# Two heads' scores on the two halves of the array's rows, one scan of 1280 columns per head, and W_in's chunks split 1024 columns at a time

## The chip, the core and the metric

The kernel runs on one core of one Trainium2 chip. The metric is the time of one execution on the device in microseconds (us); lower is better. Five engines work in parallel, each through its own list of instructions in order: PE (matmuls and transposes), ACT (activations and copies), DVE (elementwise arithmetic and scans), POOL (here masks and a few small things) and SP, which issues the DMAs. They wait for each other on semaphores only.

## What is computed

One layer of a decoder trunk with 512 tokens, width 1024, 8 heads of 64, in float32. Only the attention matters here. `q`, `k`, `v` are columns of `h @ w_in`, and each head weighs its values by stick breaking:

```python
z = einsum('bhqd,bhkd->bhqk', q, k) * 64 ** -0.5
causal = key_pos < q_pos                       # strictly
log_beta = log_sigmoid(z)
log_keep = where(causal, log_beta - z, 0.0)    # log(1 - beta)
between = cumsum(log_keep, reverse=True) - log_keep
w = where(causal, exp(log_beta + between), 0.0)
y = einsum('bhqk,bhkd->bhqd', w, v)
```

So a weight is its own `beta` times the product of all `keep = 1 - beta` that lie to its right in the same row, up to the diagonal.

## The kernel before

**Numbers in two parts.** PE reads a rounded float32 type. Every operand x of a matmul is therefore split (`split`, L63 to L66) into a high part, which ACT casts (line L64), and a low part, x minus the high one, which DVE subtracts (L65). A product is three matmuls (`mm3`, L89): high times high (L90), high times low (L91), low times high (L92).

**Weights.** W_in comes in chunks of 1024 rows by 128 columns (`wcols`). SP loads a chunk into one of 4 buffers `raw` (L71). `weights` then splits it in two halves, so ACT runs two casts `whi` of 128x512 and DVE two subtractions `wlo` of 128x512. The parts lie in a pool `wts` of 15 buffers; one that is taken again waits for whoever read or saved it last. A projection (`proj`) is 8 times 3 matmuls of 512 columns into one of the 8 PSUM banks.

**Order.** PE's and SP's lists are in the order in which the program is written (`manual_schedule`). ACT's, DVE's and POOL's lists are put in order by the framework's scheduler when the program is built.

**The attention.** The loop at L424 runs over j = 0 to 3, two heads each, which I call pair j, with heads a and b. In order, PE does: the scores of both heads, two projections for the convolution (`conv_u`, `conv_b`), the transposes of head a's weights (`wtrans`, L366), the next pair's q projection, the transposes of head b's weights, the next pair's k projection, the products with v (`av`, L380) and the next `conv_c` projection.

**Scores before** (`scores`, called once per head). `proj_q` and `proj_k` leave, for each head, a tile `st` whose 128 rows hold q's 64 high values above its 64 low values (swapped for head b), and k's high parts twice and k's low parts twice. One matmul over 128 rows thus gives two of the products, and two matmuls (L338, L339) give all four. The causal part of the scores is four blocks `BLK` of 512, 384, 128 and 256 columns, 1280 in all, in three PSUM banks. ACT takes `beta` (L341) and `keep` (L342) out of each bank. POOL sets the diagonal blocks (L347). Then, block by block, DVE forms the running product of `keep` from right to left (L350) and multiplies it into `beta` (L351), one column shifted. For each projection of k, ACT copies four pieces of 64x512 (L325) and DVE subtracts four (L326); for q two and two (L315 to L318).

**Other work in this stage.** `make_sums` loads pieces of another weight, DVE forms sums (L308), and SP saves them to DRAM (`wsum`, L291), in this stage between W_in's loads.

Of the kernel before, what the change touches and what calls it, by code (L numbers as in the profile page):

```python
# [16 lines left out]
P = 128  # L17
# [16 lines left out]
def hybrid_block(ctx, tc, x, p, g_pre_mix, w_in, b_gate, w_conv, w_attn_out, w_conv_out, w_o,  # L34
# [19 lines left out]
    def bigt(shape, dt=F32R, name="big"):  # L54
        return big.tile(shape, dt, tag="big", name=name)
# [12 lines left out]
    def weights(loads, shape):  # L68
        raw = raws.tile(shape, F32, tag="raw", name="raw")
        for sel, src in loads(raw):  # L70
            nc.sync.dma_start(sel, src)  # L71
        lo = wts.tile(shape, F32R, tag="w", name="wlo")
        hi = wts.tile(shape, F32R, tag="w", name="whi")
        half = shape[1] // 2
        for sl in (slice(0, half), slice(half, 2 * half)):
            split(hi[:, sl], lo[:, sl], raw[:, sl])
        return hi, lo
# [233 lines left out]

    def proj_q(j):
        a, b = st = [bigt([P, 3, S], name="st") for _ in range(2)]
        ps = proj(wcols(w_in, j * P), hx)
        nc.scalar.copy(a[0:64, 0], ps[0:64])  # L315
        nc.vector.tensor_tensor(a[64:128, 0], ps[0:64], a[0:64, 0].bitcast(F32), op=ALU.subtract)
        nc.scalar.copy(b[64:128, 0], ps[64:128])
        nc.vector.tensor_tensor(b[0:64, 0], ps[64:128], b[64:128, 0].bitcast(F32), op=ALU.subtract)  # L318
        return st

    def proj_k(j, st):
        ps = proj(wcols(w_in, 512 + j * P), hx)
        for s_, r, o in ((st[0], slice(0, 64), slice(64, 128)), (st[1], slice(64, 128), slice(0, 64))):
            for d in (r, o):
                nc.scalar.copy(s_[d, 1], ps[r])  # L325
                nc.vector.tensor_tensor(s_[d, 2], ps[r], s_[r, 1].bitcast(F32), op=ALU.subtract)  # L326

    def scores(st):
        beta = bigt([P, 1280], F32, "beta")
        keep = bigt([P, 1280], F32, "keep")  # L330
        for group in ((3,), (2, 0), (1,)):
            ps = bank()
            base = BLK[group[0]][0]
            for qb in group:
                c0, n = BLK[qb]
                c0 -= base
                lhs = st[:, 0, qb * P:(qb + 1) * P]
                nc.tensor.matmul(ps[:, c0:c0 + n], lhs, st[:, 1, 0:n], start=True, stop=False)  # L338
                nc.tensor.matmul(ps[:, c0:c0 + n], lhs, st[:, 2, 0:n], start=False, stop=True)  # L339
            n = sum(BLK[qb][1] for qb in group)  # L340
            nc.scalar.activation(beta[:, base:base + n], ps[:, 0:n], AF.Sigmoid, scale=0.125)  # L341
            nc.scalar.activation(keep[:, base:base + n], ps[:, 0:n], AF.Sigmoid, scale=-0.125)  # L342
        for qb in (3, 2, 0, 1):
            c0, n = BLK[qb]
            dg = slice(c0 + n - P, c0 + n)
            for t_, fill in ((beta, 0.0), (keep, 1.0)):
                nc.gpsimd.affine_select(t_[:, dg], t_[:, dg], pattern=[[-1, P]], compare_op=ALU.is_gt,  # L347
                                        fill=fill, base=0, channel_multiplier=1)
            kr = keep[:, c0:c0 + n][:, ::-1]
            nc.vector.tensor_tensor_scan(kr, kr, kr, 1.0, op0=ALU.mult, op1=ALU.bypass)  # L350
            nc.vector.tensor_tensor(beta[:, c0:c0 + n - 1], beta[:, c0:c0 + n - 1], keep[:, c0 + 1:c0 + n],  # L351
                                    op=ALU.mult)
# [71 lines left out]
    for j in range(4):  # L424
        wa = scores(st[0])
        wb = scores(st[1])
# [482 lines left out]
```

## Time and profile before

| what | value |
|---|---|
| time, median of 3 runs | 736.56 us (735.95 to 737.09) |
| time of the profiled execution | 737.48 us |
| its span, first to last instruction | 735.7 us |
| PE busy | 727.5 us, 99% of the span |
| DVE, ACT, POOL busy | 538.4, 392.4, 89.2 us |
| TensorE's granted clock | 1.000 |

How to read it: the profile is one execution. Its span is the time from the first to the last instruction; 1.8 us of the execution's own time lie around it. Start times are counted from the span's start. A row of the timeline holds start, length, engine, line, operation, out<-in by the program's names, and in brackets the idle time of the engine before it and who ended it. A matmul's length reaches until its result can be used; the next one starts earlier, so the distance of the starts is PE's pace.

### The profile page before, as it was taken

Reading aid. Unit: us, or ns where it says so; the run is one execution under the profiler, and the core shown is the slowest. Engines: PE = TensorE matmul, PEld = TensorE weight load, DVE = VectorE, ACT = ScalarE, POOL = GpSimd, SP = SyncE. Lnnn points to the kernel's source line nnn. Section 1 sums busy time; section 2 is a strip of 40 time slices with the busy share of each in tenths; the row PEclk is TensorE's granted clock in tenths of the full one; section 3 lists DMA queues with packets and bytes.
Section 4 is the critical chain, followed back from the end, with each engine's and each line's share of the span. In section 5 each row is a group of like instructions: output and inputs, shape, how many; then the busy total and the mean of one; then the engine's idle time right before and its main releaser. Section 6 shows DMA issues by size and latency. Waiting matters only on the chain.

```text
span 735.7 us, 10417 instructions
## 1 busy us (share of the span) xinstructions
PE 727.5 (99%) x3944; PEld 631.4 (86%) x3944; DVE 538.4 (73%) x740; ACT 392.4 (53%) x647; POOL 89.2 (12%) x119
## 2 busy tenths in 40 slices
PE   8999999999999999999999999999999999999997
PEld 7878888888888888888899999999988888888886
DVE  6779898989545533844789898976799878269762
ACT  6264746373434221443856696757767477256431
POOL 1005041323332222001100000000000000001100
PEclk9999999999999999999999999999999999999999
DMA  8591717174798967862325544523555767577311
GB/s 314 170 290 57 218 40 229 62 224 141 234 341 256 279 207 261 296 216 70 152 94 170 176 115 115 148 81 107 153 171 178 219 249 226 177 242 270 128 57 58
DMA packets 112106, 132.29 MB, mean 180 GB/s; under 512 B 4116, under 2 KB 82744, under 8 KB 111032
## 3 DMA queue, kind: packets, MB, share of 16 engines
q1 hardware_dynamic: 111464, 127.43, 54.8%
q10 hardware_dynamic: 592, 4.20, 1.4%
q8 instruction: 31, 0.51, 0.3%
q14 instruction: 19, 0.16, 0.1%
HBM read 108.55 MB, written 23.07 MB: 179 GB/s over the span
## 4 chain that ended last, share of the span: by engine, by line
PE 85%; DVE 6%; DMA 5%; issue 1%; ACT 1%; SPq 0%; POOL 0%; POOLq 0%; DVEq 0%; ACTq 0%
PE ps L90 27%; PE ps L92 27%; PE ps L91 26%; DMA raw<-in_w_up_dram 3%; DMA raw<-in_w_in_dram 2%; DVE us L65 2%; PE ps L380 1%; PE ps L366 1%; PE ps L339 1%; PE ps L181 1%; PE ps L338 1%; PE ps L565 1%; PE ps L140 0%; DVE s L660 0%; DVE wlo L65 0%
## 5 line engine op out<-in xcount | busy, mean ns | idle before, releaser
L65 DVE TENSOR_TENSOR wlo<-raw,whi 128x512 fp32r<-128x512 f32 x120 | 84.8, 737 | 42.7 <-ACT whi L64 20.9
L90 PE MATMUL ps<-h1h,whi 128*128 128x512 f32 x288 | 113.0, 392 | 0.0
L92 PE MATMUL ps<-h1h,wlo 128*128 128x512 f32 x288 | 112.3, 390 | 0.0
L91 PE MATMUL ps<-h1l,whi 128*128 128x512 f32 x288 | 112.2, 390 | 0.0
L64 ACT CAST whi<-raw 128x512 fp32r<-128x512 f32 x120 | 68.9, 630 | 48.5 <-DMA raw<-in_w_in_dram 15.8
L90 PE MATMUL ps<-w,sb 128*128 128x512 f32 x216 | 84.1, 389 | 0.0
L92 PE MATMUL ps<-w,sb 128*128 128x512 f32 x216 | 84.0, 389 | 0.0
L91 PE MATMUL ps<-w,sb 128*128 128x512 f32 x216 | 84.0, 389 | 0.0
L65 DVE TENSOR_TENSOR w<-raw,w 128x1024 fp32r<-128x1024 f32 x56 | 67.6, 1221 | 21.5 <-ACT w L64 10.4
L64 ACT CAST w<-raw 128x1024 fp32r<-128x1024 f32 x56 | 58.4, 1052 | 36.1 <-DMA raw<-wsum 14.4
L132 POOL TENSOR_TENSOR rs<-ms,mhalf 128x1 f32<-128x1 f32 x20 | 14.2, 712 | 419.6 <-DVE ms L128 365.7
L90 PE MATMUL ps<-h2h,us 128*128 128x256 f32 x224 | 63.5, 283 | 0.4 <-DVE tmp L692 0.4
L92 PEld LDWEIGHTS ps<-h1h,wlo 128*128 128x128 f32 x288 | 54.1, 188 | 11.3
L91 PEld LDWEIGHTS ps<-h1l,whi 128*128 128x128 f32 x288 | 54.1, 188 | 10.8
L91 PE MATMUL ps<-h2l,us 128*128 128x256 f32 x224 | 63.4, 283 | 0.0
L92 PE MATMUL ps<-h2h,us 128*128 128x256 f32 x224 | 63.4, 283 | 0.0
L90 PEld LDWEIGHTS ps<-h1h,whi 128*128 128x128 f32 x288 | 54.1, 188 | 10.8
L65 DVE TENSOR_TENSOR us<-raw,us 128x1024 fp32r<-128x1024 f32 x42 | 50.6, 1219 | 5.9 <-ACT us L64 5.8
L64 ACT CAST us<-raw 128x1024 fp32r<-128x1024 f32 x42 | 43.3, 1049 | 17.0 <-DVE raw L664 8.5
L91 PEld LDWEIGHTS ps<-w,sb 128*128 128x128 f32 x216 | 40.6, 188 | 8.4
L92 PEld LDWEIGHTS ps<-w,sb 128*128 128x128 f32 x216 | 40.6, 188 | 8.4
L90 PE MATMUL ps<-tb,us 128*128 128x256 f32 x168 | 47.7, 284 | 0.0
(210 smaller groups left out, 1693.1 us busy)
## 6 DMA issues: line engine op xcount, KB each, us to landing
raw<-in_w_in_dram SPq DMA_DIRECT2D x36, 512.0 KB, 6.5
w<-in_w_down_dram SPq DMA_DIRECT2D x32, 512.0 KB, 4.5
wsum<-w SPq DMA_DIRECT2D x32, 512.0 KB, 4.1
raw<-in_w_up_dram SPq DMA_DIRECT2D x32, 512.0 KB, 4.6
raw<-wsum SPq DMA_DIRECT2D x32, 512.0 KB, 5.0
raw<-in_w_down_dram SPq DMA_DIRECT2D x24, 512.0 KB, 4.2
raw<-in_w_o_dram SPq DMA_DIRECT2D x8, 512.0 KB, 5.7
raw<-in_w_ple_gate_dram SPq DMA_DIRECT2D x8, 512.0 KB, 7.1
```

The source lines that it names most:

```text
L64: a = nc.scalar.copy(hi, src)
L65: b = nc.vector.tensor_tensor(lo, src, hi.bitcast(F32), op=ALU.subtract)
L90: nc.tensor.matmul(ps, lh, rh, start=start, stop=False, skip_group_check=onto)
L91: nc.tensor.matmul(ps, lh, rl, start=False, stop=False, skip_group_check=onto)
L92: nc.tensor.matmul(ps, ll, rh, start=False, stop=stop, skip_group_check=onto)
L132: nc.gpsimd.tensor_tensor(r, m, mhalf, op=ALU.pow)
L181: nc.tensor.transpose(warm[:, 0:P], ident, ident)
L338: nc.tensor.matmul(ps[:, c0:c0 + n], lhs, st[:, 1, 0:n], start=True, stop=False)
L339: nc.tensor.matmul(ps[:, c0:c0 + n], lhs, st[:, 2, 0:n], start=False, stop=True)
L366: nc.tensor.transpose(ps[:, c0 + (qb - kb) * P:c0 + (qb - kb + 1) * P], w[:, o:o + P], ident)
L380: nc.tensor.matmul(ps[:, kb * P:S], lhs, wt[i][:, c0:c0 + n], start=(kb == 0 and i == 0), stop=(kb == NT - 1 and i == 1))
L565: nc.tensor.transpose(ps[:, i * P:(i + 1) * P], hn1[t][g][:, i * P:(i + 1) * P], ident)
```

## The change

Three things are changed.

1. **Scores.** The high and low parts of q and k now stay where the projection puts them: rows 0 to 63 are head a, rows 64 to 127 head b. `st` is one tile with q high, q low, k high, k low, and each projection is split once over 128 rows. A score block is three matmuls of 64 rows per head (high·high, high·low, low·high; low·low is no longer formed). `scores` is called once for both heads and issues the two heads' matmuls in turn, on the array's upper and lower rows, into two banks.
2. **Scan.** A tile `ends` holds 1.0 in the last column of each block and 0 elsewhere. One scan over all 1280 columns of a head replaces four: the running product is replaced by max(product, `ends`), and since `keep` is at most 1 and is 1 in a block's last column, it starts anew with 1 there. One multiplication of 1279 columns replaces four; what it carries over a block's edge is multiplied by a `beta` of 0.
3. **W_in's chunks** are split whole: one cast and one subtraction of 128x1024.

```diff
-    def weights(loads, shape):
+    def weights(loads, shape, parts=2):
...
-        half = shape[1] // 2
-        for sl in (slice(0, half), slice(half, 2 * half)):
+        n = shape[1] // parts
+        for i in range(parts):
+            sl = slice(i * n, (i + 1) * n)
             split(hi[:, sl], lo[:, sl], raw[:, sl])
...
-        return weights(lambda t: [(t, src)], [P, NK, P])
+        return weights(lambda t: [(t, src)], [P, NK, P], 1 if w is w_in else 2)
...
+    ends = bigt([P, 1280], F32, "ends")
+    nc.gpsimd.memset(ends, 0.0)
+    for c0, n in BLK.values():
+        nc.gpsimd.memset(ends[:, c0 + n - 1:c0 + n], 1.0)
+
     def proj_q(j):
-        a, b = st = [bigt([P, 3, S], name="st") for _ in range(2)]
-        ps = proj(wcols(w_in, j * P), hx)
-        nc.scalar.copy(a[0:64, 0], ps[0:64])
...
+        st = bigt([P, 4, S], name="st")
+        split(st[:, 0], st[:, 1], proj(wcols(w_in, j * P), hx))
         return st
 
     def proj_k(j, st):
-        ps = proj(wcols(w_in, 512 + j * P), hx)
-        for s_, r, o in ((st[0], slice(0, 64), slice(64, 128)), (st[1], slice(64, 128), slice(0, 64))):
-            for d in (r, o):
-                nc.scalar.copy(s_[d, 1], ps[r])
-                nc.vector.tensor_tensor(s_[d, 2], ps[r], s_[r, 1].bitcast(F32), op=ALU.subtract)
+        split(st[:, 2], st[:, 3], proj(wcols(w_in, 512 + j * P), hx))
 
     def scores(st):
...
+        beta = [bigt([P, 1280], F32, "beta") for _ in range(2)]
+        keep = [bigt([P, 1280], F32, "keep") for _ in range(2)]
         for group in ((3,), (2, 0), (1,)):
-            ps = bank()
+            ps = [bank(), bank()]
...
-                lhs = st[:, 0, qb * P:(qb + 1) * P]
-                nc.tensor.matmul(ps[:, c0:c0 + n], lhs, st[:, 1, 0:n], start=True, stop=False)
-                nc.tensor.matmul(ps[:, c0:c0 + n], lhs, st[:, 2, 0:n], start=False, stop=True)
+                for i, (a, b) in enumerate(((0, 2), (0, 3), (1, 2))):
+                    for h in range(2):
+                        r = slice(64 * h, 64 * h + 64)
+                        nc.tensor.matmul(ps[h][:, c0:c0 + n], st[r, a, qb * P:(qb + 1) * P], st[r, b, 0:n],
+                                         start=i == 0, stop=i == 2)
             n = sum(BLK[qb][1] for qb in group)
-            nc.scalar.activation(beta[:, base:base + n], ps[:, 0:n], AF.Sigmoid, scale=0.125)
-            nc.scalar.activation(keep[:, base:base + n], ps[:, 0:n], AF.Sigmoid, scale=-0.125)
...
+            for h in range(2):
+                nc.scalar.activation(beta[h][:, base:base + n], ps[h][:, 0:n], AF.Sigmoid, scale=0.125)
+                nc.scalar.activation(keep[h][:, base:base + n], ps[h][:, 0:n], AF.Sigmoid, scale=-0.125)
+        for h in range(2):
+            for c0, n in BLK.values():
...
-            kr = keep[:, c0:c0 + n][:, ::-1]
-            nc.vector.tensor_tensor_scan(kr, kr, kr, 1.0, op0=ALU.mult, op1=ALU.bypass)
-            nc.vector.tensor_tensor(beta[:, c0:c0 + n - 1], beta[:, c0:c0 + n - 1], keep[:, c0 + 1:c0 + n],
-                                    op=ALU.mult)
+            kr = keep[h][:, ::-1]
+            nc.vector.tensor_tensor_scan(kr, kr, ends[:, ::-1], 1.0, op0=ALU.mult, op1=ALU.max)
+            nc.vector.tensor_tensor(beta[h][:, 0:1279], beta[h][:, 0:1279], keep[h][:, 1:1280], op=ALU.mult)
         return beta
...
-        wa = scores(st[0])
-        wb = scores(st[1])
+        wa, wb = scores(st)
```

Three lists that the scheduler orders come out as follows. In the changed program the activations are lines L343 and L344, the masks L349, the scan L352 and the product L353.

ACT before, pair 0, the last six activations (of head b) and what follows, with the semaphores that each waits for; DMAHW0 to DMAHW7 tell of landed DMAs and are used in turn:

```order
L341 ACTIVATE beta<-ps 128x512 [waits PE_49,Activation_49]
L342 ACTIVATE keep<-ps 128x512 [waits Activation_49]
L341 ACTIVATE beta<-ps 128x512 [waits PE_49]
L342 ACTIVATE keep<-ps 128x512
L341 ACTIVATE beta<-ps 128x256 [waits PE_49]
L342 ACTIVATE keep<-ps 128x256
L64 CAST whi<-raw 128x512 [waits DMAHW2_49]
L64 CAST whi<-raw 128x512
L64 CAST whi<-raw 128x512 [waits DMAHW6_49,DMAHW3_49]
```

ACT now, pair 0, from the cast ahead of the scores to the first pair of 256 columns (head a's):

```order
L64 CAST whi<-raw 128x1024 [waits DMAHW2_49,DVE_49]
L343 ACTIVATE beta<-ps 128x512 [waits PE_49]
L344 ACTIVATE keep<-ps 128x512
L343 ACTIVATE beta<-ps 128x512 [waits PE_49,Activation_49]
L344 ACTIVATE keep<-ps 128x512 [waits Activation_49]
L64 CAST whi<-raw 128x1024 [waits DMAHW6_49,DMAHW3_49]
L343 ACTIVATE beta<-ps 128x512 [waits PE_49]
L344 ACTIVATE keep<-ps 128x512
L343 ACTIVATE beta<-ps 128x512 [waits PE_49]
L344 ACTIVATE keep<-ps 128x512
L343 ACTIVATE beta<-ps 128x256 [waits PE_49]
L344 ACTIVATE keep<-ps 128x256
```

The cast that waits for DMAHW6 (the landing of the second of the two saves `wsum` behind the first twelve chunks) and DMAHW3 (its own chunk, the eleventh) stood behind all twelve activations; it now stands behind the first four of them. In pairs 1 and 2 a cast of 1024 stands at the same place; in pair 3 none does.

POOL before, pair 1 (`beta_868`, `keep_869` are head a's, 911 and 912 head b's):

```order
L347 AFFINE_SELECT beta_868<-beta_868 128x128
L347 AFFINE_SELECT keep_869<-keep_869 128x128
L347 AFFINE_SELECT beta_868<-beta_868 128x128 x2
L347 AFFINE_SELECT keep_869<-keep_869 128x128 x2
L347 AFFINE_SELECT beta_868<-beta_868 128x128
L347 AFFINE_SELECT keep_869<-keep_869 128x128
L347 AFFINE_SELECT beta_911<-beta_911 128x128
L347 AFFINE_SELECT keep_912<-keep_912 128x128
```

POOL now, pair 1 (836 and 838 are head a's, 837 and 839 head b's):

```order
L349 AFFINE_SELECT beta_836<-beta_836 128x128
L349 AFFINE_SELECT keep_838<-keep_838 128x128
L349 AFFINE_SELECT beta_837<-beta_837 128x128
L349 AFFINE_SELECT keep_839<-keep_839 128x128
L349 AFFINE_SELECT beta_836<-beta_836 128x128 x2
L349 AFFINE_SELECT keep_838<-keep_838 128x128 x2
L349 AFFINE_SELECT beta_837<-beta_837 128x128 x2
L349 AFFINE_SELECT keep_839<-keep_839 128x128 x2
L349 AFFINE_SELECT beta_836<-beta_836 128x128
L349 AFFINE_SELECT keep_838<-keep_838 128x128
L349 AFFINE_SELECT beta_837<-beta_837 128x128
L349 AFFINE_SELECT keep_839<-keep_839 128x128
```

Head a's last mask of `keep` was the eighth of sixteen and is now the fourteenth.

DVE before, pair 1, from the last chunk's subtractions ahead of the scan (the scan is printed as SCALAR_TENSOR_TENSOR):

```order
L65 TENSOR_TENSOR wlo_1312<-raw_1310,whi_1313 128x512 x2
L350 SCALAR_TENSOR_TENSOR keep_869<-keep_869 128x512
L351 TENSOR_TENSOR beta_868<-beta_868,keep_869 128x511
L350 SCALAR_TENSOR_TENSOR keep_869<-keep_869 128x384
L350 SCALAR_TENSOR_TENSOR keep_869<-keep_869 128x128
L351 TENSOR_TENSOR beta_868<-beta_868,keep_869 128x383
L351 TENSOR_TENSOR beta_868<-beta_868,keep_869 128x127
L350 SCALAR_TENSOR_TENSOR keep_869<-keep_869 128x256
L350 SCALAR_TENSOR_TENSOR keep_912<-keep_912 128x512
L351 TENSOR_TENSOR beta_868<-beta_868,keep_869 128x255
```

DVE now, pair 1:

```order
L65 TENSOR_TENSOR wlo_1289<-raw_1287,whi_1290 128x1024
L352 SCALAR_TENSOR_TENSOR keep_838<-keep_838,ends_383 128x1280
L352 SCALAR_TENSOR_TENSOR keep_839<-keep_839,ends_383 128x1280
L353 TENSOR_TENSOR beta_836<-beta_836,keep_838 128x1279
L353 TENSOR_TENSOR beta_837<-beta_837,keep_839 128x1279
L398 TENSOR_TENSOR tmp_834<-tmp_834,ps_924 128x512
L65 TENSOR_TENSOR wlo_1345<-raw_1343,whi_1346 128x1024
```

Head a's product, which its transposes on PE read, stood behind head a's scans and the first of head b's; it now stands behind both heads' whole scans.

More of the change, by code (lines that the diff above doesn't have):

```diff
@@ new lines, in scores @@
+            n = sum(BLK[qb][1] for qb in group)
+            for h in range(2):
[3 more added lines that the diff above has]
+            for c0, n in BLK.values():
+                dg = slice(c0 + n - P, c0 + n)
+                for t_, fill in ((beta[h], 0.0), (keep[h], 1.0)):
+                    nc.gpsimd.affine_select(t_[:, dg], t_[:, dg], pattern=[[-1, P]], compare_op=ALU.is_gt,
+                                            fill=fill, base=0, channel_multiplier=1)
+            kr = keep[h][:, ::-1]
+            nc.vector.tensor_tensor_scan(kr, kr, ends[:, ::-1], 1.0, op0=ALU.mult, op1=ALU.max)
+            nc.vector.tensor_tensor(beta[h][:, 0:1279], beta[h][:, 0:1279], keep[h][:, 1:1280], op=ALU.mult)
```

11 lines of the change are left out of this document (removed).

## The prediction, made before the changed kernel ran

> **What bounds the kernel now.** I read the page first: which engine is busy throughout, and what the chain that ended last is made of.
>
> ```profile
> span 735.7 us, 10417 instructions
> PE 727.5 (99%) x3944; PEld 631.4 (86%) x3944; DVE 538.4 (73%) x740; ACT 392.4 (53%) x647; POOL 89.2 (12%) x119
> PE 85%; DVE 6%; DMA 5%; issue 1%; ACT 1%; SPq 0%; POOL 0%; POOLq 0%; DVEq 0%; ACTq 0%
> ```
>
> PE is busy for 99% and makes 85% of the chain. So a part of the change counts only by the time at which PE starts something, and DVE or ACT work counts where PE would wait for it. Next the windows of a pair: busy time by engine in the scores, then from there to head a's transposes, for pair 0 (second row) and pair 1.
>
> ```profile
> 57.37:68.30 10.93, 10.93 (x51) 8.96 (x50) 10.52 (x18) 6.83 (x16) 9.12 (x15) 1.00 0.01 3
> 89.42:91.96 2.54, 2.54 (x17) 2.37 (x16) 1.61 (x3) 2.34 (x5) 0.77 (x3) 1.00 1.07 398
> 91.96:102.89 10.93, 10.93 (x50) 8.97 (x49) 10.43 (x18) 6.49 (x15) 8.55 (x14) 1.00 0.05 19
> ```
>
> The columns behind the stretch are PE, weight loads, DVE, ACT, POOL, clock, DMA share. PE needs 2.54 us for a pair's scores and 10.93 for two projections, and then reads head a's weights. In those 10.93 us DVE is busy for 10.43: PE is the bound, with DVE close behind it. The timeline of PE gives the places, pair 1 and then pair 0.
>
> ```profile
> 89.42 0.39 PE L338 MATMUL ps<-st 128*128 128x512 f32 x1
> 89.65 0.39 PE L339 MATMUL ps<-st 128*128 128x512 f32 x1
> 91.96 0.39 PE L90 MATMUL ps<-h1h,whi 128*128 128x512 f32 x1
> 102.89 1.25 PE L366 MATMUL ps<-ident,beta 128*128 128x128 f32 x10
> 103.90 0.48 PE L90 MATMUL ps<-h1h,whi 128*128 128x512 f32 x1
> ...
> 52.82 0.51 PE L338 MATMUL ps<-st 128*128 128x512 f32 x1
> 55.50 0.50 PE L338 MATMUL ps<-st 128*128 128x512 f32 x1 [0.64 <-ACT st L325]
> 57.37 0.40 PE L90 MATMUL ps<-h1h,whi 128*128 128x512 f32 x1
> 68.30 1.25 PE L366 MATMUL ps<-ident,beta 128*128 128x128 f32 x10
> ```
>
> I call the first score matmul T and head a's first transpose W. W lies 13.47 us behind T in pair 1 (102.89 − 89.42) and 15.48 in pair 0, where the scores take 4.55 instead of 2.54 because k's pieces come late. W is the place to watch: behind it PE again runs without a gap. How early are the weights there? DVE's last product of head a in pair 1 is the first of the two that this row of DVE's timeline begins:
>
> ```profile
> 97.96 0.44 DVE L351 TENSOR_TENSOR beta<-beta,keep 128x255 f32<-128x255 f32 x1
> ```
>
> It ends at 98.40, 4.5 us ahead of W. That is all the cover that the change may use up.
>
> **The change: PE.** Before, each head takes two passes over the 1280 columns, four passes in 2.54 us, 0.635 each. Now there are six passes of 64 rows. If the two heads run side by side, three passes last, 1.90 us; if one after the other, six, 3.81. Nothing in this trace runs on half the rows, so these are the two ends. I take 1.90: the two matmuls of a step share neither rows nor bank. PE would then reach W at T + 1.90 + 10.93 = 12.83; by the other end, at 14.74. In pair 0 the late k pieces go too: six casts and six subtractions become two of each.
>
> [...]
>
> **The change: what W now waits for.** Head a's product now needs one long scan, which needs the masks of all blocks, which need all activations of head a, and those now stand between head b's. The chain of pair 1, step by step, from these rows of ACT, POOL and DVE:
>
> ```profile
> 89.62 0.59 ACT L392 COPY tmp<-ps 128x512 f32<-128x512 f32 x1 [1.32 <-PE ps L92]
> 90.14 0.60 ACT L341 ACTIVATE beta<-ps 128x512 f32<-128x512 f32 x1
> 90.63 0.59 ACT L342 ACTIVATE keep<-ps 128x512 f32<-128x512 f32 x1
> 92.06 0.41 ACT L341 ACTIVATE beta<-ps 128x256 f32<-128x256 f32 x1
> 92.33 0.43 ACT L342 ACTIVATE keep<-ps 128x256 f32<-128x256 f32 x1
> ...
> 90.80 0.30 POOL L347 TENSOR_SCALAR_AFFINE_SELECT beta<-beta 128x128 f32<-128x128 f32 x1 [24.32 <-ACT beta L341]
> 91.29 0.29 POOL L347 TENSOR_SCALAR_AFFINE_SELECT keep<-keep 128x128 f32<-128x128 f32 x1 [0.19 <-ACT keep L342]
> 91.78 1.15 POOL L347 TENSOR_SCALAR_AFFINE_SELECT beta<-beta 128x128 f32<-128x128 f32 x1 [0.20 <-ACT beta L341]
> 93.68 0.54 POOL L347 TENSOR_SCALAR_AFFINE_SELECT keep<-keep 128x128 f32<-128x128 f32 x2
> ...
> 91.62 1.23 DVE L350 TENSOR_TENSOR_SCAN keep<-keep 128x512 f32<-128x512 f32 x1 [0.93 <-POOL keep L347]
> 92.88 0.69 DVE L351 TENSOR_TENSOR beta<-beta,keep 128x511 f32<-128x511 f32 x1
> ```
>
> ```profile
> L64 ACT CAST w<-raw 128x1024 fp32r<-128x1024 f32 x56 | 58.4, 1052 | 36.1 <-DMA raw<-wsum 14.4 <-PE ps L92 11.5 <-DMA raw<-in_w_down_dram 5.9
> L350 DVE TENSOR_TENSOR_SCAN keep<-keep 128x512 f32<-128x512 f32 x8 | 10.0, 1249 | 2.9 <-POOL keep L347 2.9
> L350 DVE TENSOR_TENSOR_SCAN keep<-keep 128x384 f32<-128x384 f32 x8 | 8.2, 1021 | 1.7 <-POOL keep L347 1.7
> L350 DVE TENSOR_TENSOR_SCAN keep<-keep 128x256 f32<-128x256 f32 x8 | 5.7, 715 | 0.0
> L350 DVE TENSOR_TENSOR_SCAN keep<-keep 128x128 f32<-128x128 f32 x8 | 3.6, 446 | 0.0
> L351 DVE TENSOR_TENSOR beta<-beta,keep 128x511 f32<-128x511 f32 x8 | 5.8, 725 | 0.1
> L351 DVE TENSOR_TENSOR beta<-beta,keep 128x127 f32<-128x127 f32 x8 | 2.5, 315 | 0.0
> ```
>
> 1. ACT. The copy of conv_c started 0.20 us behind T (89.62), behind PE's last matmul. Now a cast of 1024 that waits for the matmul before that one stands ahead of it, so it starts about at T. It lasts 1.05 and holds ACT for 0.94, since ACT starts the next instruction some 0.11 before an end (90.14 + 0.60 against 90.63). Copy at 0.92, then activations from 1.43, 0.48 apart (90.14, 90.63): four, to 3.36. Then the cast of 1024 that the scheduler put there, 0.94; four more from 4.30; then head a's two of 256 columns at 6.23 and 6.50, 0.27 apart (92.06, 92.33). All relative to T.
> 2. POOL. A mask starts 0.66 behind the start of its activation (90.14, 90.80), and queued masks follow every 0.25 to 0.27 (two in 0.54). From 4.96 there are eight masks of the second group, then head a's last two: the ten end at about 7.5. DVE has no scan to disturb them by then.
> 3. DVE. The scan of 1280 columns: the rows rise by (1249 − 446) / 384 = 2.09 ns a column, so 1249 + 768 · 2.09 = 2.85 us. No row shows this length, nor a maximum as the second operation. The ends are 3.43, the sum of the four rows, and 1.55, the price of a product of that width (next point); I take 2.85, on the line of four rows. First scan 7.53 to 10.38.
> 4. POOL again. Head b's last mask is caught by that scan. The mask of 91.78 took 1.15 us and ended at 92.93, 0.08 behind DVE's scan (92.85). So the second scan starts at 10.5 and ends at 13.35.
> 5. DVE. Head a's product stands behind both scans: (725 − 315) / 384 = 1.07 ns a column, 725 + 768 · 1.07 = 1.55 us; 14.85. W at T + 14.9.
>
> So W waits about 2.1 us for DVE, and it comes 14.9 − 13.47 = 1.43 us later than before. This holds for pairs 1 and 2, and PE's saving in the scores is swallowed whole by the wait. Pair 3 has no cast between the activations: 0.94 less, T + 13.96, +0.49.
>
> Pair 0. There the cast between the activations waits for the second save `wsum`, which is DMA's last work for some time:
>
> ```profile
> 57.00:58.00 1.00, 1.00 (x8) 0.91 (x7) 0.81 (x2) 1.00 (x4) 0.93 (x4) 1.00 0.15 59
> 58.00:59.00 1.00, 1.00 (x6) 0.78 (x6) 1.00 (x1) 1.00 (x5) 1.00 (x1) 1.00 0.00 0
> ```
>
> The DMA share is 0.15 in this microsecond and 0 in the next, so the save has landed by 58.0. T is 52.82 as before (conv_c sets it). The cast would run at T + 3.36 = 56.2 and runs at 58.05 instead, 1.87 later, and behind it on ACT wait eight activations, with them masks, scans, product and W. W = 52.82 + 14.9 + 1.87 = 69.6, against 68.30: +1.3. The 2.0 us that PE gains in the scores of pair 0 are lost in this wait too.
>
> **What costs nothing.** DVE's six subtractions for q and k become two, each chunk's two become one, and the scans of a head shrink from 3.43 to 2.85. None of it brings PE forward, since DVE idles ahead of the scan, waiting for masks. Switching the array between 128 and 64 rows, twice a pair, falls into the time ahead of W and is covered by the 2.1 us; without that cover it is what one switch costs, for which the nearest rows are PE's own steps, a few tenths. `ends` is written by POOL long ahead, while it idles (24.32 us of idle time ahead of one mask, above). Behind W, DVE has the second head's product, the convolution's four steps, eight subtractions, a chunk or two and some sums before head b's `av`; at 0.7 us for 512 columns and 1.2 to 1.5 for 1024 to 1280 that is some 13 us. PE takes about as long for what lies between, two groups of transposes (102.89 to 103.90, 1.01 each) and two projections (half of 10.93 each), 12.9, and head a's `av`. That is tight and is a rival below.
>
> **Sum.** 1.3 + 1.43 + 1.43 + 0.49 = +4.65 us on the profiled execution: span 735.7 to 740.3, its own time 737.48 to 742.1. The median of the runs is 0.9 below that execution, so I forecast 736.56 + 4.65 = **741.2**. Behind the attention PE is the bound again and carries the shift to the end.
>
> **Rivals.**
> - *The halves don't run side by side.* Six passes, 3.81 us: PE reaches W at T + 14.74, still ahead of 14.9 in pairs 0 to 2; in pair 3 it costs 1.27 instead of 0.49. Sum +5.4, 742.0. The change then doesn't do what it says, and the time hardly shows it; the starts of PE's matmuls would.
> - *The scan runs at a column per cycle* (the other side). At a product's price, 1.55, each of the two scans ahead of W is 1.3 shorter: W's data at T + 12.3, PE at 12.83, and PE sets the time: −0.64 in pairs 1 to 3. In pair 0 the data is there at 69.6 − 2.6 = 67.0, −1.3. Sum −3.2, 733.3. It decides once the scan takes less than about 2.1 us. Against it: four rows on one line at 2.09 ns, while products have 1.07. [...]
> - *The waits cancel.* If the cast ahead runs before T and the last mask isn't caught, W is some 1.3 earlier in each pair, and the sum is about 0, 736.6.
> - *DVE falls behind after W.* If its 13 us need 15, or its scans cost 3.43 (W 1.15 later), each pair loses 1.0 to 1.15 more: +4.65 + 4.6 = 9.3, 745.8.
>
> **How the numbers follow.** Forecast 0.60; not side by side 0.14; DVE behind 0.08; cancel 0.07; fast scan 0.11. A measurement of this kernel can tell about 0.2%, 1.5 us, from no change. Slower by over that: 0.60 + 0.14 + 0.08 = 0.82; within: 0.07; faster: 0.11. The range takes in the forecast, the serial case and the long scan up to 746, and downward a part of the cancelling case, to 737.5.
>
> **What would show it.** PE's largest new wait is for DVE, at the first transpose of each pair (L367): about 2 us in pairs 1 and 2, 1 in pair 3, near 4 in pair 0, and none at the second transposes. The scan row of 1280 near 2855 ns, the product near 1545. In pair 0 ACT idles at a cast between activations until about 58. Score matmuls side by side would start two in the time of one, and the scores take 1.9 us. The forecast is wrong if the scan is near 1.5 us, if W shows no wait, or if the wait at W is far longer than the chain above, which would mean a mask or activation later than I have it.

## The result, and the profile after

| what | before | after |
|---|---|---|
| time, median (range) of 5 runs each | 736.56 us (735.95 to 737.23) | 743.66 us (741.12 to 744.07) |
| time and span of the profiled execution | 737.48, 735.7 us | 744.07, 742.3 us |
| PE busy | 727.5 us, 99% | 727.5 us, 98% |
| DVE, ACT, POOL busy | 538.4, 392.4, 89.2 us | 517.5, 378.7, 83.5 us |
| mean granted clock of TensorE | 1.000 | 0.997 |

After over before is 1.0089, 95% interval 1.0071 to 1.0108: the change makes the kernel slower by 0.9%, although DVE has 21 us and ACT 14 us less to do. The forecast was 741.2, in a range that ends at 746.0.

The page of the changed kernel, its span, its busy times and the chain that ended last:

```profile
span 742.3 us, 10314 instructions
PE 727.5 (98%) x3976; PEld 629.4 (85%) x3976; DVE 517.5 (70%) x640; ACT 378.7 (51%) x595; POOL 83.5 (11%) x124
PE 87%; DVE 5%; POOL 3%; DMA 2%; issue 2%; ACT 1%; SPq 0%; POOLq 0%; DVEq 0%; ACTq 0%
```

PE's waits in the attention (20 to 200 us), with their sum, number and longest, and PE's timeline at the first transposes of pairs 0 and 1 and the second ones of pair 0:

```profile
PE ps L367 <- DVE beta L353: 7.3, 4, 3.8
```

```profile
52.61 2.19 PE L339 MATMUL ps<-st 64*128 64x512 f32 x24
54.74 0.50 PE L91 MATMUL ps<-h1h,whi 128*128 128x512 f32 x1
69.68 2.37 PE L367 MATMUL ps<-ident,beta 128*128 128x128 f32 x10 [3.76 <-DVE beta L353]
...
77.78 1.25 PE L367 MATMUL ps<-ident,beta 128*128 128x128 f32 x10
...
92.44 2.19 PE L339 MATMUL ps<-st 64*128 64x512 f32 x24
...
107.22 1.28 PE L367 MATMUL ps<-ident,beta 128*128 128x128 f32 x10 [1.48 <-DVE beta L353]
```

With T the first score matmul and W head a's first transpose, W lies 17.07 us behind T in pair 0 (69.68 − 52.61) and 14.78 in pair 1 (107.22 − 92.44). PE waits there for DVE's product in all four pairs, and nowhere else in this stage. One thing was not forecast: the ten transposes of pair 0 last 2.37 us instead of 1.25, and the second transposes follow the first by 8.10 us instead of 6.56 as before.

The end of the chain that W waits for, in pair 1: POOL's last masks on `keep` of heads a and b, then DVE's two scans (one row of two) and two products, then all scans and all products of the kernel.

```profile
99.52 0.30 POOL L349 TENSOR_SCALAR_AFFINE_SELECT keep<-keep 128x128 f32<-128x128 f32 x1
...
100.01 2.82 POOL L349 TENSOR_SCALAR_AFFINE_SELECT keep<-keep 128x128 f32<-128x128 f32 x1
```

```profile
99.86 5.83 DVE L352 TENSOR_TENSOR_SCAN keep<-keep,ends 128x1280 f32<-128x1280 f32 x2 [4.50 <-POOL keep L349]
105.61 2.87 DVE L353 TENSOR_TENSOR beta<-beta,keep 128x1279 f32<-128x1279 f32 x2
```

```profile
L352 DVE TENSOR_TENSOR_SCAN keep<-keep,ends x8: 2825/2856/2887, 62.3 to 174.1; 128x1280 f32<-128x1280 f32 x8
L353 DVE TENSOR_TENSOR beta<-beta,keep x8: 1465/1475/1485, 68.1 to 178.2; 128x1279 f32<-128x1279 f32 x8
```

Head a's last mask ends at 99.82 and its scan starts at 99.86, T + 7.42. Head b's last mask lasts 2.82 us instead of 0.30: it started 0.15 us into the first scan and ends about with it. Head b's scan follows, and only then head a's product (the last two rows give least, median and greatest length in ns).

### The profile page after: what moved, and what is told of

Its sections match the earlier page's. It is cut to its first block, busy times and chain, and to the rows that moved or that the text cites. A ratio compares the mean times of both kernels' runs of the same rounds, so it can differ in the third digit from the quotient of the medians.

```text
span 742.3 us, 10314 instructions
## 1 busy us (share of the span) xinstructions
PE 727.5 (98%) x3976; PEld 629.4 (85%) x3976; DVE 517.5 (70%) x640; ACT 378.7 (51%) x595; POOL 83.5 (11%) x124
## 4 chain that ended last, share of the span: by engine, by line
PE 87%; DVE 5%; POOL 3%; DMA 2%; issue 2%; ACT 1%; SPq 0%; POOLq 0%; DVEq 0%; ACTq 0%
PE ps L91 27%; PE ps L92 27%; PE ps L93 27%; POOL keep L349 2%; DVE keep L352 2%; PE ps L367 1%; DMA raw<-in_w_up_dram 1%; PE ps L381 1%; POOL beta L349 1%; DVE us L65 1%; DVE beta L353 1%; DMA wsum<-w 1%; PE ps L182 1%; PE ps L565 1%; PE ps L141 0%
## 5 line engine op out<-in xcount | busy, mean ns | idle before, releaser
L65 DVE TENSOR_TENSOR wlo<-raw,whi 128x512 fp32r<-128x512 f32 (+1 forms) x84 | 79.8, 974 | 52.8 <-ACT whi L64 32.5
L64 ACT CAST whi<-raw 128x512 fp32r<-128x512 f32 (+1 forms) x84 | 65.3, 805 | 56.7 <-DMA raw<-in_w_in_dram 14.9
L133 POOL TENSOR_TENSOR rs<-ms,mhalf 128x1 f32<-128x1 f32 x20 | 14.9, 745 | 418.9 <-DVE ms L129 365.0
```

The costliest lines, as they stand in the source:

```text
L64: a = nc.scalar.copy(hi, src)
L65: b = nc.vector.tensor_tensor(lo, src, hi.bitcast(F32), op=ALU.subtract)
L133: nc.gpsimd.tensor_tensor(r, m, mhalf, op=ALU.pow)
```

## The experiments

All were timed with the kernel before beside them on the same chip; its medians there lie between 735.74 and 736.12 us. Ratios are to it.

| label | edit | median, us | ratio (95%) |
|---|---|---|---|
| e5_again | changed kernel, as it is | 743.26 | 1.0100 (1.0086 to 1.0113) |
| e9_before_again | kernel before, as it is | 736.05 | 1.0004 (0.9993 to 1.0014) |
| e3_order | head a's product before head b's scan | 738.60 | 1.0036 (1.0024 to 1.0047) |
| e2_serial | score matmuls head after head; the cast moves too | 738.05 | 1.0029 (1.0017 to 1.0040) |
| e12_one_scan_mended | both of these | 734.89 | 0.9982 (0.9973 to 0.9990) |
| e4_scans4 | four scans per head again | 736.09 | 1.0004 (0.9994 to 1.0014) |
| e7_four_late_cast | four scans, and as e2 | 734.81 | 0.9983 (0.9975 to 0.9992) |
| e8_scan_alone | kernel before with the single scan | 740.26 | 1.0056 (1.0040 to 1.0071) |
| e11_split_alone | kernel before with W_in split whole | 735.90 | 0.9996 (0.9984 to 1.0007) |
| e10_halves | changed kernel with W_in in halves | 742.88 | 1.0090 (1.0063 to 1.0118) |
| e1_fill | 26 idle transposes in pair 0's wait | 743.31 | 1.0095 (1.0078 to 1.0112) |
| e6_fill8 | 8 of them | 742.96 | 1.0095 (1.0081 to 1.0108) |

### Is it the order of product and scan? (e3_order)

```diff
+        prod = None
         for h in range(2):
...
-            nc.vector.tensor_tensor_scan(kr, kr, ends[:, ::-1], 1.0, op0=ALU.mult, op1=ALU.max)
-            nc.vector.tensor_tensor(beta[h][:, 0:1279], beta[h][:, 0:1279], keep[h][:, 1:1280], op=ALU.mult)
+            with tc.issue_after(prod.ins) if prod else nullcontext():
+                nc.vector.tensor_tensor_scan(kr, kr, ends[:, ::-1], 1.0, op0=ALU.mult, op1=ALU.max)
+            prod = nc.vector.tensor_tensor(beta[h][:, 0:1279], beta[h][:, 0:1279], keep[h][:, 1:1280], op=ALU.mult)
```

`issue_after` keeps head b's scan behind head a's product in DVE's list.

> The changed kernel with head a's product on DVE ahead of head b's scan. Theory (the second scan in front of the product is what makes PE wait): head a's data 2.86 us earlier, T + 11.9 in pairs 1 and 2, so PE reaches its transposes at T + 13.06 with no wait; pair 0 at 66.8 with a wait of about 1.1 and a clock of 1.000. Sum against before: -1.5 in pair 0 and -0.4 in each other pair, 733.8, if nothing else gets late. Rival (DVE is the bound behind the first transposes, so what is won there is lost ahead of the second ones): PE waits 1.5 to 2 us for DVE between first and second transposes, and the time is 738 or more.

PE's waits in the attention (lines are two further down), and PE's timeline behind the first transposes of pair 0:

```profile
PE ps L91 <- DVE tmp L410: 1.5, 1, 1.5
PE ps L91 <- DVE wtl L65: 0.7, 2, 0.3
PE ps L369 <- DVE beta L355: 0.6, 1, 0.6
```

```profile
76.26 0.50 PE L91 MATMUL ps<-h1h,whi 128*128 128x512 f32 x1 [1.53 <-DVE tmp L410]
```

The theory was right about the first transposes: the wait there is gone but for 0.6 us in pair 0 (W at 66.85, forecast 66.8). Its time, 733.8, was wrong: DVE now has head b's scan and product behind W and is late with the convolution's product (L410), for which PE waits 1.5 us. That is the rival's loss and its time, though the wait stands behind the second transposes and not ahead of them. 738.60 is 5 us better than the changed kernel and 2.7 worse than before.

### Is it the cast between the activations? (e2_serial)

```diff
-                for i, (a, b) in enumerate(((0, 2), (0, 3), (1, 2))):
-                    for h in range(2):
+                for h in range(2):
+                    for i, (a, b) in enumerate(((0, 2), (0, 3), (1, 2))):
```

> The changed kernel with the score matmuls of a group issued head after head instead of alternating, so that no two that can run side by side are neighbours but at the joints; the scheduler then also puts the cast that stood between the activations behind them. Theory (side by side saves 1.9 us of PE, but the chain through DVE sets head a's transposes): scores take 3.8 to 4.0 us instead of 2.13; the chain is 0.94 shorter and no longer waits for the save in pair 0, so data at T + 14.0, PE at T + 14.9 to 15.1 and no wait for DVE there; pair 0 at 67.6 instead of 69.68 with no fall of the clock. Sum against the kernel before: -0.7 in pair 0, +1.5 in each other pair: +3.8, about 740.3, less than the changed kernel although PE does its scores slower. Rival (the halves were not side by side in the changed kernel): scores still 2.1 us, waits of about 0.9 at the transposes, sum about 0, 736.5.

Windows of the scores in pairs 0 and 1 (length, then busy time of PE, weight loads, DVE, ACT, POOL, clock, DMA share), and PE's waits:

```profile
53.01:55.14 2.13, 2.13 (x26) 1.88 (x25) 1.16 (x1) 2.03 (x4) 0.00 (x0) 1.00 1.09 376
89.08:91.22 2.14, 2.14 (x26) 1.88 (x25) 1.78 (x2) 2.14 (x4) 0.16 (x1) 1.00 0.45 172
```

```profile
PE ps L367 <- DVE beta L353: 3.1, 4, 1.5
```

PE's first two score matmuls of pair 1, in the changed kernel and then in e2:

```profile
92.44 0.50 PE L339 MATMUL ps<-st 64*128 64x512 f32 x2
89.08 0.50 PE L339 MATMUL ps<-st 64*128 64x512 f32 x2
```

The theory was wrong about the scores: issued head after head they take 2.13 us too, as when alternating. So this kernel doesn't undo the side by side. The rival's reading, that there was none, is wrong as well: two matmuls of 512 columns start together and take 0.50 us in either kernel, and 24 matmuls that by the forecast's count would need 3.81 us one after the other finish in 2.13. In e2 the two can only be head a's first and head b's first, since two of 512 columns on the same rows start 0.23 us apart (89.42 and 89.65 in the kernel before); so head b's first, fourth in the list, starts ahead of head a's second. What the kernel does test is the cast. In pair 0 of the changed kernel it stood there:

```profile
55.60 0.62 ACT L344 ACTIVATE keep<-ps 128x512 f32<-128x512 f32 x1
58.17 1.05 ACT L64 CAST whi<-raw 128x1024 fp32r<-128x1024 f32 x1 [1.95 <-DMA wsum<-w]
59.12 0.59 ACT L343 ACTIVATE beta<-ps 128x512 f32<-128x512 f32 x1
```

ACT idles 1.95 us, casts for 0.95, and the second group's activations come only then. With the cast behind them W comes at T + 14.79 in pair 0 (67.80 − 53.01), 2.3 us earlier than in the changed kernel, and in pairs 1 and 2 some 0.95 earlier, at T + 13.83 (102.91 and 137.98, from T at 89.08 and 124.15), as the chain of steps has it. Pair 0 keeps 0.96 more than these, largely because POOL's masks are late there: one of them takes 1.29 us (from 56.67) beside a subtraction on DVE (56.59 to 57.81). The time is 738.05, against the 740.3 expected.

### Both together, and four scans (e4_scans4, e7_four_late_cast, e12_one_scan_mended)

e4 puts the four scans and products back into the loop over the blocks:

```diff
-            kr = keep[h][:, ::-1]
-            nc.vector.tensor_tensor_scan(kr, kr, ends[:, ::-1], 1.0, op0=ALU.mult, op1=ALU.max)
-            nc.vector.tensor_tensor(beta[h][:, 0:1279], beta[h][:, 0:1279], keep[h][:, 1:1280], op=ALU.mult)
+                kr = keep[h][:, c0:c0 + n][:, ::-1]
+                nc.vector.tensor_tensor_scan(kr, kr, kr, 1.0, op0=ALU.mult, op1=ALU.bypass)
+                nc.vector.tensor_tensor(beta[h][:, c0:c0 + n - 1], beta[h][:, c0:c0 + n - 1],
+                                        keep[h][:, c0 + 1:c0 + n], op=ALU.mult)
```

e7 is e4 with e2's edit, e12 the changed kernel with e2's and e3's.

> The changed kernel with four scans and four products per head as before, the scores side by side and W_in's chunks in one piece as changed. Theory (the loss comes from the single scan, which starts only after all masks, and from the order of the two heads around it): scans start as soon as each block's masks are there, head a's data is ready before PE, no wait at the first transposes in pairs 1 to 3 (T + 13.06), W in pair 0 at 66 to 67; sum between -1.3 and -3.8, 732.8 to 735.3. Rival (the loss comes from the activations of the two heads in turn and the cast between them): waits of 1 us or more at the first transposes stay, time 739 or more.

> The changed kernel with four scans and four products per head as before, and the score matmuls of a group issued head after head, which makes the scheduler put the cast behind all activations; the scores stay side by side. Theory (side by side wins 0.4 us a pair at PE once DVE starts early enough and no cast stands between the activations): first transposes at T + 13.15 in every pair without a wait, second ones 6.6 to 7.1 later; against before -2.0 in pair 0 and -0.2 in each other pair, about 733.3. Rival (DVE is the bound behind the first transposes, as with the other order of product and scan): waits of 0.5 to 1.5 us come back behind them, 736 to 738.

> The changed kernel, with its single scans, with both orders mended: head a's product ahead of head b's scan, and the cast behind the activations (through score matmuls issued head after head). Theory (the loss is the order on ACT and DVE, not the length of the scan): first transposes at T + 13.15 without a wait in all pairs; DVE starts 0.9 us earlier than where only the product was moved, so the waits behind the transposes, 1.8 us in pair 0 and 0.6 to 0.7 in the next two, shrink to under 0.5; 734.5 to 736. Rival (one scan instead of four makes DVE start too late, since it idles while masks are made, and it is late behind the first transposes whatever the order): waits of 0.5 to 1.5 us between the second transposes and the next scores in each pair, 736.5 to 738.5, against 734.81 with four scans.

e4 comes out as before (736.09, ratio 1.0004), a little above what was expected; two waits of some 0.7 us for the last blocks' products (L348) remain within the transposes. e7 and e12 beat both kernels, e7 by less than expected (733.3): that sum counted pair 0 from the first profile of before, which is long there (below). PE's waits in e7 and then in e12, from 20 us to 740 us:

```profile
PE ps L363 <- DVE beta L348: 0.2, 1, 0.2
```

```profile
PE ps L91 <- DVE tmp L410: 0.4, 1, 0.4
```

And the stretch from the scores' end to W in pair 0 of e12, with DVE's rows in it:

```profile
55.16:66.19 11.03, 11.03 (x51) 9.07 (x50) 6.92 (x4) 6.52 (x14) 7.43 (x16) 1.00 0.12 45
```

```profile
60.47 2.89 DVE L354 TENSOR_TENSOR_SCAN keep<-keep,ends 128x1280 f32<-128x1280 f32 x1 [2.40 <-POOL keep L350]
63.39 1.49 DVE L355 TENSOR_TENSOR beta<-beta,keep 128x1279 f32<-128x1279 f32 x1
64.80 2.82 DVE L354 TENSOR_TENSOR_SCAN keep<-keep,ends 128x1280 f32<-128x1280 f32 x1
```

Head a's data is ready at 64.88, 1.3 us ahead of PE, and W comes at T + 13.16. So with both orders mended the single scan costs nothing: it is as fast as four (734.89 and 734.81), and both are 1.1 to 1.2 us faster than before. Not all of that need be PE's saving in the scores: the attention (second transposes of pair 3) ends at 176.28 in e7 and 176.65 in e12, only 0.6 and 0.3 us ahead of the second profile of the kernel before (176.91), and 2.4 and 2.0 ahead of its first (178.64). The rival of e12, that DVE starts too late with one scan, holds for 0.6 us in pair 0 (second transposes to next scores: 15.28 us, against 14.65 in e7) and hardly in the others.

### One part at a time (e8_scan_alone, e11_split_alone, e10_halves)

e8 puts the scan of 1280 columns and `ends` into the kernel before, e11 the `parts` of W_in; e10 takes `, 1 if w is w_in else 2` out of the changed kernel.

> The kernel before with one scan and one product of 1280 columns per head as the only change: scores head after head on all 128 rows, W_in in halves. Theory (the long scan costs nothing where the heads come one after the other, since head a's product follows its scan at once): first transposes at T + 13.5 without a wait, as before; some DVE work is late behind them, 0 to 1.2 us in a pair; 736 to 738.5. Rival (the long scan alone makes PE wait at the first transposes): waits of 1 us or more there in each pair and 740 or more.

> The kernel before with W_in's chunks cast and subtracted in one piece of 1024 as the only change. Theory (it takes its price only where a cast stands on the chain that PE waits for): head a's data is ready 4.5 us ahead of PE in the kernel before, so nothing is waited for at the transposes; 735.3 to 737.3. Rival (whole chunks come late, since a cast of 1024 ends later than the first half did): waits for W_in in the projections, 738 or more.

> The changed kernel with W_in's chunks split in halves as before, so that casts are 512 wide. Theory (the cast between the activations is a part of the chain ahead of the first transposes): only one cast of 512 stands there, 0.5 us instead of 0.94, so the waits at the first transposes of pairs 1 and 2 fall from 1.45 to about 1.0 and T to W from 14.78 to 14.3; in pair 0 the cast still waits for the save and W stays within 0.5 us of 69.5; 741.7 to 742.7. Rival (the width of the split has no part in it): waits of 1.45 as before, 743 to 744.

- e11: no wait for DVE at any transpose, 735.90, no difference. The split costs nothing by itself.
- e8: as the theory has it, no wait at the first transposes. But the waits behind them, expected at up to 1.2 us a pair, are more: in pairs 1 and 2 `av` waits for a late low part of the weights, and from second transposes to next scores it takes 16.04 and 16.06 us instead of 14.57 in the second profile of before. That is 3.0 us. At the second transposes of pair 3 its profile is 4.3 us behind that of before (181.19 and 176.91); the other 1.3 arise in pair 0, where the scores take 4.06 us instead of 2.71 (see the late k pieces below). 740.26, 4.3 above before, is outside the expectation. So alone, in the order of before, the single scan does cost time, by making DVE late behind the transposes; e12, where it costs nothing, also leaves DVE fewer subtractions, and which difference makes the room is not shown.

```profile
PE ps L384 <- DVE wtl L65: 2.0, 2, 1.0
```

- e10 misses its expectation: T to W in pair 1 is 14.65 instead of 14.78, not 14.3. The cast between the activations is 0.44 shorter, but the scheduler now puts both halves of the cast ahead (1.14 us) before the activations, which start at T + 1.63 instead of 1.32. In pair 2 T to W is 15.66, because there too the cast between the activations waits for a save `wsum` (ACT idles 0.90 us; 0.22 in the second profile of the changed kernel, with T to W 15.10), and in pair 0 W comes at 68.65. The time, 742.88, with runs from 740.32 to 744.39, tells nothing.

### Where is the rest of the loss? (e9_before_again, e5_again, e1_fill, e6_fill8)

By the first profile of before, W's shifts alone give less than was measured. Two things come into question: the base, and the long transposes of pair 0.

> The kernel before as it is, for a second profile of it: its first one, 737.48 us, lies above most of its runs. Theory (the difference between runs of one kernel arises outside the attention, in waits for loads): first and second transposes of the four pairs within 0.5 us of the first profile, and where the span is 734 the 1.5 us are saved behind the attention. Rival (it arises in the attention): the transposes of pair 3 come 1 us earlier or more.

The windows from T to W in pair 0 of the second profile of the kernel before, and then ACT's rows ahead of the scores in the first and in the second:

```profile
52.94:55.65 2.71, 2.71 (x17) 2.35 (x16) 2.03 (x4) 2.48 (x5) 0.67 (x2) 1.00 1.06 384
55.65:66.57 10.92, 10.92 (x51) 8.97 (x50) 10.52 (x18) 6.81 (x16) 9.11 (x15) 1.00 0.06 23
```

```profile
51.02 1.14 ACT L64 CAST whi<-raw 128x512 fp32r<-128x512 f32 x2 [1.92 <-DMA raw<-in_w_in_dram]
52.19 0.58 ACT L325 CAST st<-ps 64x512 fp32r<-64x512 f32 x1
```

```profile
49.30 1.14 ACT L64 CAST whi<-raw 128x512 fp32r<-128x512 f32 x2
50.47 0.58 ACT L325 CAST st<-ps 64x512 fp32r<-64x512 f32 x1
```

This execution has a span of 733.6, against 735.7 in the first. T is 0.1 us later, but the scores of pair 0 take 2.71 us instead of 4.55, and W comes at 66.57 instead of 68.30. The rival was right: 1.73 of the 2.1 us arise in the attention. In the first profile a cast of a W_in chunk waited 1.92 us for its load, k's pieces stood behind it on ACT, and PE waited for them. How late it is differs from execution to execution: the scores of pair 0 take 4.06 in e8 and 3.54 in e11 (whose casts are 1024 wide), and there too the cast ahead of k's second piece waits for its load, 1.13 and 1.18 us.

For the long transposes:

```diff
+        if j == 0:
+            fb = bank()
+            for i in range(26):
+                nc.tensor.transpose(fb[:, 0:P], ident, ident)
         ta = wtrans(wa)
```

> The changed kernel as it is, a second profile and more times, on the same chip as the kernels run with it. Theory (the fall of the clock costs 1.6 us, and a run without it is that much shorter): executions with a mean clock of 1.000 near 741.5, those with 0.996 to 0.998 near 743.5. Rival (the 743.3 at a clock of 1.000 in the kernel with 26 transposes shows that the time does not hang on the clock): both kinds of execution at 743 to 744.

> The changed kernel with 26 transposes of the identity into a bank that nobody reads, ahead of head a's first transposes in pair 0 alone, so that PE works through most of its wait of 3.76 us there. Theory (the wait makes the granted TensorE clock fall, and that costs 1.6 us behind it): head a's first transposes stay at 69.7 us, since DVE sets them; the second transposes follow 6.6 us later (as in the kernel before) instead of 8.1; mean clock 1.000 instead of 0.997; span 740.7, times near 742. Rival (the transposes are slow there for another reason, such as DVE or PSUM being busy beside them): still 8.1 us, clock 0.997, times near 743.7.

> The changed kernel with 8 transposes of the identity instead of 26 in the wait of pair 0, which leaves a wait of about 2.8 us. Theory (the clock falls only where PE idles for longer than some time between 1.5 us, after which it did not fall in pairs 1 and 2, and 3.76 us): clock 1.000 in pair 0 and 6.6 us from first to second transposes if that time is above 2.8 us, 8.1 us or near it if it is below. Rival (the loss grows in step with the wait): about 7.7 us.

Windows of 1 us around W in pair 0 of the changed kernel (W at 69.68), and of its second profile (W at 69.31, after a wait of 2.99), each with the stretch at half clock as its last row; the clock is the third number from the end:

```profile
69.00:70.00 1.00, 0.32 (x2) 0.35 (x3) 1.00 (x2) 0.00 (x0) 0.00 (x0) 0.70 0.00 0
70.00:71.00 1.00, 1.00 (x7) 1.00 (x6) 1.00 (x2) 0.00 (x0) 0.00 (x0) 0.50 0.00 0
71.00:72.00 1.00, 1.00 (x6) 1.00 (x6) 1.00 (x2) 0.00 (x0) 0.00 (x0) 0.50 0.00 0
72.00:73.00 1.00, 1.00 (x5) 0.76 (x4) 1.00 (x2) 0.00 (x0) 0.00 (x0) 0.59 0.00 0
73.00:74.00 1.00, 1.00 (x6) 0.83 (x5) 0.96 (x3) 0.00 (x0) 0.00 (x0) 1.00 0.00 0
69.40:72.81 3.41, 3.13 (x13) 2.97 (x14) 3.41 (x5) 0.00 (x0) 0.00 (x0) 0.50 0.00 0
```

```profile
69.00:70.00 1.00, 0.69 (x7) 0.72 (x8) 1.00 (x2) 0.00 (x0) 0.00 (x0) 1.00 0.01 4
70.00:71.00 1.00, 1.00 (x8) 0.91 (x7) 1.00 (x2) 0.00 (x0) 0.00 (x0) 0.72 0.00 0
71.00:72.00 1.00, 1.00 (x4) 0.80 (x3) 1.00 (x2) 0.00 (x0) 0.00 (x0) 0.50 0.00 0
72.00:73.00 1.00, 1.00 (x4) 0.71 (x4) 0.96 (x3) 0.00 (x0) 0.00 (x0) 0.50 0.00 0
73.00:74.00 1.00, 1.00 (x4) 0.81 (x3) 1.00 (x2) 0.00 (x0) 0.00 (x0) 0.57 0.00 0
70.44:73.85 3.41, 3.41 (x11) 2.64 (x10) 3.38 (x6) 0.00 (x0) 0.00 (x0) 0.50 0.00 0
```

First to second transposes of pair 0 in the changed kernel, and in e1 and e6 one after the other:

```profile
69.68:77.78 8.10, 8.10 (x34) 6.97 (x35) 7.27 (x10) 1.31 (x3) 0.00 (x0) 0.81 0.01 2
```

```profile
69.69:76.29 6.60, 6.60 (x35) 5.58 (x35) 6.46 (x8) 0.00 (x0) 0.00 (x0) 1.00 0.01 2
```

```profile
69.71:76.31 6.60, 6.60 (x34) 5.58 (x35) 6.46 (x8) 0.00 (x0) 0.00 (x0) 1.00 0.01 2
```

The granted clock is 0.50 for 3.41 us, from 69.40 in the first profile and from 70.44 in the second, and nowhere else in the attention. With the wait filled (e1) or cut to 2.51 us (e6), W is where it was, since DVE sets it, the clock stays at 1.00 and the stretch lasts 6.60 instead of 8.10. In the traces the cause is shown: the long wait costs 1.5 us beside its own length. It agrees in size with the half clock: PE works for 3.13 of the 3.41 us, and half of that is 1.57.

The half clock came after waits of 3.76 and 2.99 us (the two profiles of the changed kernel), and not after 2.51 (e6) or 2.32 (e10).

In the measured times the gain of the two fills is small: 743.31 and 742.96 against 743.66 and 743.26, where near 742 was expected of e1. The attention of e1 ends 1.6 us earlier than that of the changed kernel (second transposes of pair 3 at 183.49 against 185.05), but its profile then loses 2 us far behind it: the waits of e1's PE and DVE, PE from 440 to 560 us, DVE from 440 to 500.

```profile
PE ps L91 <- DVE tmp L696: 2.1, 2, 1.6
```

```profile
DVE s L664 <- DMA raw<-in_w_up_dram: 9.4, 6, 3.5
```

DVE waits for a piece of another weight, and PE for DVE. The same waits are 0.6 and 7.5 us in the changed kernel's first profile, and 0.7 and 7.7 in e6. On the other hand, among the nine executions of the changed kernel that were timed, the two with a mean clock of 1.000 took 741.12 and 742.24, and the seven with 0.994 to 0.998 took 743.17 to 744.23. What the clock's fall is worth in the median, between 0.3 and 2 us, and why e1 loses at those loads, stays open.

## Why the prediction was right, and where its size was off

The sign, the place and the mechanism were right; the time, 743.66, lies 2.5 above the forecast. That it still lies in the range is in part luck: the room up to 746 was left for serial scores and a slower scan, and neither came. By its steps, all from T in pair 1 (T = 92.44):

| step | forecast | measured |
|---|---|---|
| scores | 1.90 | 2.13 |
| first activation | 1.43 | 1.32 |
| last mask of head a | 7.5 | 7.38 |
| first scan starts | 7.53 | 7.42 |
| scan, product | 2.85, 1.55 | 2.856, 1.475 |
| second scan ends | 13.35 | 13.25 |
| W | 14.9 | 14.78 |
| W in pair 3 (no cast between) | 13.96 | 13.94 |

- **Side by side** was the author's choice between two values, since no row of before runs on 64 rows. It held: two matmuls of 512 columns start at 92.44 and take 0.50 us together. But PE gains less than the 0.64 us a pair of the forecast. The scores take 2.13 us instead of 1.90, and some 0.1 more goes ahead of them (14.65 us from the second transposes in e7, 14.56 before) and behind them (11.03 to W in e12, 10.93 before). From the second transposes of pair 0 to W of pair 1, without a wait in either, e7 is 0.22 faster than the second profile of before (27.81 and 28.03). In the trace of pair 1 PE's steps are longer at the two changes between 128 and 64 rows: 0.32 us into the first score matmuls (92.12 to 92.44), 0.34 behind them (to 92.78), 0.21 from the last ones, of 256 columns, into the projection (94.36 to 94.57) and 0.33 behind that (to 94.90). In the kernel before the same four steps take 0.22, 0.23, 0.11 and 0.23 (89.20 to 89.42 and 89.65, 91.85 to 91.96 and 92.19), together 0.41 less. Why they are longer, no run takes apart. As forecast, all this is covered by the wait.
- **The caught mask** (2.82 us) and **the product behind both scans** came as said, and e3 shows that the order is worth 5 us.
- **The rivals.** The serial halves and the fast scan are out by the rows above. DVE doesn't fall behind after W in the changed kernel; it does as soon as W comes earlier (e3). The two waits that would have cancelled did not.
- **The step that was mis-sized** is pair 0's term: "W = 52.82 + 14.9 + 1.87 = 69.6, against 68.30: +1.3". The 69.6 was right (69.68), but the 68.30 is not a fixed time of the kernel. It held late k pieces, seen as scores of 4.55 us where the second profile has 2.71, and W came 1.73 us later by it; against the second profile the term is 69.68 − 66.57 = 3.1. The same lateness is most of the 2.1 us between the two profiles, and the prediction took the first one's surplus over the median off both kernels alike ("The median of the runs is 0.9 below that execution, so I forecast 736.56 + 4.65"). In the changed kernel the scores of pair 0 take 2.13 us in both profiles and DVE sets W, so its median has no such lateness to lose; that this is why the surplus doesn't come off it is argued, not tested. The "2.0 us that PE gains in the scores of pair 0" are the late k pieces alone; with 1.90 for the scores it would have been 2.65. That figure is not in the sum.
- **The term that was missing** is the clock. A wait "near 4" us in pair 0 was forecast, and what PE does after such a wait was not asked: 1.5 us in the trace.

Against the second profile of before, the shift at the second transposes of pair 3 (176.91 to 185.05) is made up so, in us:

| term | forecast | measured |
|---|---|---|
| W of pair 0 | 1.3 | 3.1 |
| clock behind it | – | 1.5 |
| pairs 1 and 2, from the second transposes ahead to W | 1.43 each | 1.41 each |
| pair 3, likewise | 0.49 | 0.56 |
| all else | – | 0.1 |
| sum | 4.65 | 8.1 |

From T to W alone pairs 1 and 2 lose 1.31 each (14.78 and 13.47); the other 0.1 lies ahead of T. Against the first profile the sum is 6.4 (178.64 to 185.05). The medians differ by 7.1, which lies between.

## What to carry to other kernels

Work that is saved on three engines counts for nothing if the one result that the bound engine waits for moves to the end of a longer queue: look at which instruction each list puts ahead of that result (here another head's scan, and a cast that itself waited for a DMA), and mend the order before judging the edit. Where a profiled execution is slower than the median, find out where its surplus lies; if a new wait will stand over that place, the surplus can't be taken off both sides. And a forecast wait of some microseconds on TensorE is to be priced with what follows it (here 1.5 us at a clock of 0.50 behind a wait of 3.76), not with its length alone.

## What the hardware showed that was not expected

- After waits of 3.76 and 2.99 us TensorE's granted clock fell to 0.50 for 3.41 us; after 2.51 it did not. In the first profile it fell 0.28 us ahead of the wait's end, in the second only at 70.44, when PE had been working again for 1.1 us.
- Matmuls on the two row halves ran side by side in either order of issue: 2.13 us for a pair's scores when alternating, 2.13 and 2.14 when three of one head were issued ahead of three of the other. Of these last, the two that start together at 89.08 in e2 can only be the first head's first and the second head's first, so the latter started ahead of two that stood before it in PE's list.
